# The last two of sixteen batches transposed by the DMA crossbar instead of TensorE

## Chip, cores, metric

One core of one Trainium2 chip. The metric is the device time of one execution in microseconds (us), as the runs report it.

## The reference

RWKV time mixing on x of 16 x 2048 x 256 (batch, sequence, model), fp32. Cut to what matters (the key branch is computed by the reference but never reaches the output):

```python
x_prev[:, 1:, :] = x[:, :-1, :]                  # the token before, zero for the first
xv = x * time_mix_v + x_prev * (1 - time_mix_v)
xr = x * time_mix_r + x_prev * (1 - time_mix_r)
v = xv @ value_weight
r = xr @ receptance_weight
out = (1 / (1 + exp(-r)) * v) @ output_weight
```

## The kernel before

The 32,768 tokens are worked in 64 units of 512, four to a batch. SBUF and PSUM are the two on-chip memories. For a unit, TensorE transposes x (tokens on partitions) so that the model dimension lies on partitions, ScalarE copies the result from PSUM to SBUF, VectorE and GpSimd mix each column with the column of the token before (a scale by a per-partition coefficient, then an add), and TensorE projects. The token before is in the neighbouring slot of 128 columns, which is why `xt` has one slot more than the batch; that first slot is filled by a "slot copy".

```python
def transposes(i):                       # runs LOOK = 6 units ahead
    ...
    ps = ps_t_pool.tile([P, KO, TU], BF16, name="ps_t")
    for ko in range(KO):                 # 8 TensorE transposes a unit
        one(ps[:, ko], ko, src, idn)
    nc.scalar.copy(out=xt[b][:, :, c0 : c0 + TU], in_=ps)
...
for g in range(NU - 1):                  # NU = 64 units
    project(ps_r, g, 0)                              # TensorE
    nc.scalar.activation(out=s_sb, in_=ps_r, func=ACT.Sigmoid)
    advance(START_T[g] if g < len(START_T) else g + LOOK)   # loads, transposes
    for p in products.get(g + 1, []):
        if g + LOOK >= NU and p[0][1] == 1:
            scale_act(p[0], (0,))        # value scale of a pair of units on ScalarE
    ...                                  # otherwise scales and adds on VectorE
    project(ps_v, g, 1)                              # TensorE
    nc.vector.tensor_tensor(out=z_sb, in0=s_sb, in1=ps_v, op=ALU.mult)
    for p in pooled[g]:
        scale_pool(p, last)              # the other half of the scales, GpSimd
    ...
    output(g - 1, z_prev)                # TensorE, copy on ScalarE, store by Sync
```

## Time and profile before

| | before |
|---|---|
| median of four runs | 212.62 us (212.14 to 213.71) |
| span of the profiled execution | 211.2 us |
| TensorE, VectorE, ScalarE busy | 96%, 91%, 89% of the span |
| pace in the middle | 3.046 us a unit |

A share of busy time says that three engines are nearly full, not which of them sets the pace. That is read from the idle time in front of each group of instructions; the prediction shows those lines. It also shows what units without TensorE transposes cost: 2.695 us, in the last units of this very kernel.

### The profile page before, as it was taken

How to read it: one execution, taken by the hardware profiler on the slowest of the kernel's cores; microseconds unless marked ns; L12 is line 12 of the kernel's file. 1: busy time of each engine (PE TensorE's matmuls, PEld its weight loads, DVE VectorE, ACT ScalarE, POOL GpSimd, SP SyncE). 2: the span in 40 equal slices, each digit the busy share in tenths (PEclk: the TensorE clock that was granted, in tenths of full speed). 3: DMA queues.
4: the chain of work that ended last, by engine and by line, in shares of the span. 5: the costliest groups of instructions: out<-in, count | busy, mean ns of one | idle time of the engine just before them, and what ended most of it. 6: DMA issues, size and time to landing. Idle time of an engine off the chain costs nothing.

```text
span 211.2 us, 4188 instructions
## 1 busy us (share of the span) xinstructions
PE 201.8 (96%) x1562; PEld 134.6 (64%) x1589; DVE 192.0 (91%) x314; ACT 187.2 (89%) x206; POOL 78.7 (37%) x108
## 2 busy tenths in 40 slices
PE   8879999999999999999999999999999999999991
PEld 7456665666666666666666666666666666665570
DVE  2869999999999999999999999999999999999962
ACT  3669999999999999999999999999999999999891
POOL 2623231544344425433452444335344432444200
PEclk9999999999999999999999999999999999999998
DMA  5999999999999897998989999898999944433475
GB/s 181 281 214 221 215 265 238 319 219 292 270 250 273 273 230 326 192 354 174 298 228 236 337 194 352 157 317 231 242 304 203 371 202 202 199 143 154 202 300 202
DMA packets 10284, 52.04 MB, mean 246 GB/s; under 512 B 1044, under 2 KB 2328, under 8 KB 5144
## 3 DMA queue, kind: packets, MB, share of 16 engines
q0 software_dynamic: 3008, 16.12, 44.2%
q1 hardware_dynamic: 7104, 35.52, 41.4%
q8 instruction: 12, 0.20, 0.4%
q10 hardware_dynamic: 152, 0.13, 0.2%
q14 instruction: 8, 0.07, 0.1%
HBM read 34.34 MB, written 33.55 MB: 322 GB/s over the span
## 4 chain that ended last, share of the span: by engine, by line
PE 79%; DVE 7%; DMA 5%; issue 4%; ACT 2%; POOL 1%; SPq 0%; DVEq 0%; POOLq 0%
PE psum_o L298 23%; PE psum_v L274 22%; PE psum_r L274 21%; PE ps_t L189 11%; DMA x_unit<-in_x_dram 5%; DVE mix L263 3%; DVE mix L239 2%; ACT s_sb L501 2%; DVE z_sb L527 1%; POOL mix L250 1%; PE ps_t L298 1%; ACT xt_first L206 0%; PE ps_t L274 0%; DVE xt_first L402 0%; DVE z_sb L359 0%
## 5 line engine op out<-in xcount | busy, mean ns | idle before, releaser
L250 POOL TENSOR_SCALAR mix<-xt,c_sb 128x1024 bf16<-128x1024 bf16 (+1 forms) x55 | 61.1, 1111 | 100.9 <-DVE mix L263 98.8
L527 DVE TENSOR_TENSOR z_sb<-s_sb,psum_v 128x1024 bf16<-128x1024 bf16 x63 | 76.7, 1218 | 4.7 <-PE psum_v L274 2.5
L263 DVE TENSOR_TENSOR mix<-mix,xt 128x1024 bf16<-128x1024 bf16 x112 | 78.0, 699 | 2.6
L330 ACT COPY o_sb<-psum_o 128x1024 f32<-128x1024 f32 x61 | 62.0, 1016 | 11.7 <-PE psum_o L298 11.7
L274 PEld LDWEIGHTS <-w_bf 128*128 128x128 bf16 x516 | 47.9, 98 | 33.8 <-issue 1.1
L501 ACT ACTIVATE s_sb<-psum_r 128x1024 bf16<-128x1024 f32 x63 | 65.1, 1034 | 0.5 <-PE psum_r L274 0.2
L274 PE MATMUL psum_v<-mix,w_bf 128*128 128x512 bf16 (+1 forms) x246 | 64.3, 377 | 0.8 <-DVE z_sb L527 0.2
L298 PE MATMUL psum_o<-wo_bf,z_sb 128*128 128x256 bf16 x498 | 64.8, 273 | 0.2
L274 PE MATMUL psum_r<-mix,w_bf 128*128 128x512 bf16 (+1 forms) x236 | 62.8, 377 | 0.6
L298 PEld LDWEIGHTS <-z_sb 128*128 128x128 bf16 x512 | 49.9, 98 | 20.2 <-DVE z_sb L359 1.2
L206 ACT COPY xt<-ps_t 128x1024 bf16<-128x1024 bf16 x56 | 57.0, 1022 | 0.0
L189 PEld LDWEIGHTS <-x_bf 128*128 128x128 bf16 x488 | 32.1, 98 | 13.5
L189 PE MATMUL ps_t<-ident,x_bf 128*128 128x128 bf16 x488 | 36.7, 219 | 0.2
L239 DVE TENSOR_SCALAR mix<-xt,c_sb 128x1024 bf16<-128x1024 bf16 (+1 forms) x59 | 26.9, 463 | 0.0
L263 DVE TENSOR_TENSOR mix<-mix,xt_first 128x1024 bf16<-128x1024 bf16 x15 | 10.2, 687 | 0.1
L250 POOL TENSOR_SCALAR mix<-xt_first,c_sb 128x512 bf16<-128x512 bf16 x6 | 4.1, 690 | 13.0 <-DVE xt_first L402 10.8
L106 POOL DMA_DIRECT2D x_bf<-in_x_dram x14 | 8.1, 582 | 0.0
L239 DVE TENSOR_SCALAR mix<-xt_first,c_sb 128x512 bf16<-128x512 bf16 x22 | 6.6, 349 | 0.2
L206 ACT COPY xt_first<-ps_t 128x1024 bf16<-128x1024 bf16 x5 | 5.2, 1033 | 0.0
L199 ACT CAST xt_first<-ps_t 128x512 bf16<-128x512 f32 x4 | 2.1, 589 | 3.3 <-PE ps_t L189 3.3
L140 PE MATMUL ps_t<-zeros 128*128 128x128 bf16 x38 | 3.8, 275 | 1.0 <-DVE zeros L84 1.0
L140 PEld LDWEIGHTS <-zeros 128*128 128x128 bf16 x38 | 3.2, 126 | 1.0 <-DVE zeros L84 1.0
(64 smaller groups left out, 43.4 us busy)
## 6 DMA issues: line engine op xcount, KB each, us to landing
out_dram<-o_sb SPq DMA_DIRECT2D x30, 1024.0 KB, 7.8
x_bf<-in_x_dram POOLq DMA_DIRECT2D x14, 1024.0 KB, 11.1
x_bf<-in_x_dram POOLq DMA_DIRECT2D x5, 256.0 KB, 8.8
x_unit<-in_x_dram SPq DMA_DIRECT2D x2, 512.0 KB, 6.3
out_dram<-o_sb SPq DMA_DIRECT2D x4, 256.0 KB, 2.1
x_unit<-in_x_dram SPq DMA_DIRECT2D x2, 256.0 KB, 3.0
out_dram<-o_sb SPq DMA_DIRECT2D x1, 512.0 KB, 2.6
out_dram<-o_sb SPq DMA_DIRECT2D x3, 128.0 KB, 2.7
```

What stands on the lines that cost most here:

```text
L106: nc.gpsimd.dma_start(out=x_bf[b], in_=rows(b))
L140: nc.tensor.matmul(out=ps, lhsT=zeros, rhs=zeros, start=True, stop=True)
L189: nc.tensor.transpose(out=ps[:, jj * P : (jj + 1) * P], in_=src[:, jj, ko * P : (ko + 1) * P], identity=idn,)
L206: nc.scalar.copy(out=xt[b][:, :, c0 : c0 + TU], in_=ps)
L239: nc.vector.tensor_scalar(out=mix[b][:, m, ko, lo:hi], in0=xt[b][:, ko, c : c + hi - lo], scalar1=c_sb[:, m, ko : ko + 1], scalar2=None, o ...
L250: op = nc.gpsimd.tensor_scalar(out=mix[b][:, m, 1, lo:hi], in0=xt[b][:, 1, c : c + hi - lo], scalar1=c_sb[:, m, 1:2], scalar2=1.0, op0=ALU ...
L263: return nc.vector.tensor_tensor(out=mix[b][:, m, :, lo:hi], in0=mix[b][:, m, :, lo:hi], in1=xt[b][:, :, c : c + hi - lo], op=ALU.add,)
L274: nc.tensor.matmul(out=ps[:, mo, :], lhsT=w_bf[:, m, ko, mo * P : (mo + 1) * P], rhs=mix[b][:, m, ko, e * TU + lo : e * TU + hi], start=(k ...
L298: nc.tensor.matmul(out=ps[:, slot, :], lhsT=z[:, ko, jj * P : (jj + 1) * P], rhs=wo_bf[:, ko, :], start=(ko == 0), stop=(ko == KO - 1),)
L330: nc.scalar.copy(out=o_sb[b][:, j0 : j0 + UJ, :], in_=ps)
L501: nc.scalar.activation(out=s_sb, in_=ps_r, func=ACT.Sigmoid)
L527: nc.vector.tensor_tensor(out=z_sb, in0=s_sb, in1=ps_v, op=ALU.mult)
```

## The change

Intent: TensorE sets the pace, and 0.45 us of each unit is transposes. Near the end the loads are done and the DMA engines have time, so the last two batches (units 56 to 63) are transposed by a DMA, SBUF to SBUF, one instruction for each batch (`dma_start_transpose`, called the crossbar below). The DMA writes block by block (token slot, then half of the model dimension), so `xt` and `mix` get that order in all batches. Batches 14 and 15 must lie whole in SBUF earlier, hence a fourth input buffer and loads two units earlier; to make room the first units' input shares an output buffer. ScalarE, rid of its copies, takes the value scale in those units.

```diff
+    BYDMA = 2
-    xpool = ctx.enter_context(tc.tile_pool(name="xpool", bufs=3))
+    xpool = ctx.enter_context(tc.tile_pool(name="xpool", bufs=4))
-    x_unit = consts.tile([P, 3, UJ, D], FP32)
+    x_unit = opool.tile([P, 3, UJ, D], FP32, name="o_sb")
-            xt[b] = xtpool.tile([P, KO, (J + 1) * P], BF16, name="xt")
+            xt[b] = xtpool.tile([P, J + 1, KO, P], BF16, name="xt")
+    def by_dma(b):
+        new_xt(b)
+        late_copies.append((b, UB - 1))
+        nc.sync.dma_start_transpose(
+            out=xt[b][:, 1:].rearrange("p j k c -> p (j k) c"),
+            in_=x_bf[b].rearrange("p j d -> p (j d)"),
+        )
... (all access patterns follow the new order)
-            if e == 1 and 2 < b + 2 < B:
-                load(b + 2)
-            transposes(tnext)
+            if e == UB - 1 and b + 3 < B:
+                load(b + 3)
+            if b < B - BYDMA:
+                transposes(tnext)
...
+        if g % UB == 0 and B - BYDMA <= g // UB + 2 < B:
+            by_dma(g // UB + 2)
-            if g + LOOK >= NU and p[0][1] == 1:
+            if g + LOOK >= NU - BYDMA * UB and p[0][1] == 1:
```

More of the change, by code (lines that the diff above doesn't have):

```diff
@@ L145, in new_xt @@
         if b < BYUNIT:
-            xt[b] = consts.tile([P, KO, UB * (UJ + 1) * P], BF16, name=f"xt_first{b}")
+            xt[b] = consts.tile([P, UB * (UJ + 1), KO, P], BF16, name=f"xt_first{b}")
         else:
-            xt[b] = xtpool.tile([P, KO, (J + 1) * P], BF16, name="xt")
-        (nc.vector if b == 0 else nc.gpsimd).memset(xt[b][:, :, 0:1], 0.0)
+            xt[b] = xtpool.tile([P, J + 1, KO, P], BF16, name="xt")
+        (nc.vector if b == 0 else nc.gpsimd).memset(xt[b][:, 0, :, 0:1], 0.0)
     new_xt(0)
@@ L182, in transposes, with one @@
             e = (e - 1) % UB
-        c0 = (1 + e * UJ + (e if b < BYUNIT else 0)) * P
+        j0 = 1 + e * UJ + (e if b < BYUNIT else 0)
         if b < BYUNIT or e == UB - 1:
             late_copies.append((b, e))
-        def one(ps, ko, src, idn):
-            for jj in range(UJ):
-                nc.tensor.transpose(
-                    out=ps[:, jj * P : (jj + 1) * P],
-                    in_=src[:, jj, ko * P : (ko + 1) * P],
-                    identity=idn,
-                )
+        def one(ps, jj, ko, src, idn):
+            nc.tensor.transpose(
+                out=ps[:, jj], in_=src[:, jj, ko * P : (ko + 1) * P], identity=idn
+            )
         if i in (1, 2):
             for ko in range(KO):
-                ps = ps_t_pool.tile([P, TU], FP32, name="ps_t")
-                one(ps, ko, x_unit[:, i], ident_f)
-                nc.scalar.copy(out=xt[b][:, ko, c0 : c0 + TU], in_=ps)
+                ps = ps_t_pool.tile([P, UJ, P], FP32, name="ps_t")
+                for jj in range(UJ):
+                    one(ps, jj, ko, x_unit[:, i], ident_f)
+                nc.scalar.copy(out=xt[b][:, j0 : j0 + UJ, ko, :], in_=ps)
             return
-        ps = ps_t_pool.tile([P, KO, TU], BF16, name="ps_t")
+        ps = ps_t_pool.tile([P, UJ, KO, P], BF16, name="ps_t")
         src = x_bf3 if b == 0 else x_bf[b][:, e * UJ : (e + 1) * UJ, :]
-        idn = ident
-        for ko in range(KO):
-            one(ps[:, ko], ko, src, idn)
-        nc.scalar.copy(out=xt[b][:, :, c0 : c0 + TU], in_=ps)
+        for jj in range(UJ):
+            for ko in range(KO):
+                one(ps[:, :, ko], jj, ko, src, ident)
+        nc.scalar.copy(out=xt[b][:, j0 : j0 + UJ], in_=ps)
     def first_transposes():
         def half(h, pool, name):
-            ps = pool.tile([P, KO, TU], FP32, name=name)
-            for ko in range(KO):
-                for jj in range(H):
+            ps = pool.tile([P, UJ, KO, P], FP32, name=name)
+            for jj in range(H):
+                for ko in range(KO):
                     nc.tensor.transpose(
-                        out=ps[:, ko, jj * P : (jj + 1) * P],
+                        out=ps[:, jj, ko],
                         in_=x_unit[:, 0, h * H + jj, ko * P : (ko + 1) * P],
@@ L217, in half @@
                     )
-            c0 = (1 + h * H) * P
-            nc.scalar.copy(out=xt[0][:, :, c0 : c0 + H * P], in_=ps[:, :, 0 : H * P])
+            nc.scalar.copy(out=xt[0][:, 1 + h * H : 1 + h * H + H], in_=ps[:, 0:H])
         pl = ps_t_pool.tile([P, KO, P], FP32, name="ps_t")
@@ L225, in first_transposes, with slots, mixed @@
             )
-        nc.vector.tensor_copy(out=xt[0][:, :, 1:P], in_=pl[:, :, 0 : P - 1])
+        nc.vector.tensor_copy(out=xt[0][:, 0, :, 1:P], in_=pl[:, :, 0 : P - 1])
         half(1, ps_r_pool, "psum_r")
         half(0, ps_v_pool, "psum_v")
-    def columns(piece):
-        b, _, lo, _ = piece
-        return lo + (lo // TU) * P if b < BYUNIT else lo
+    def slots(piece, off=0):
+        b, _, lo, hi = piece
+        j = lo // P + (lo // TU if b < BYUNIT else 0) + off
+        return slice(j, j + (hi - lo) // P)
+    def mixed(piece):
+        b, m, lo, hi = piece
+        return mix[b][:, m, lo // P : hi // P]
     def scale(piece, kos=(0, 1)):
-        b, m, lo, hi = piece
-        c = columns(piece)
+        b, m, _, _ = piece
         for ko in kos:
             nc.vector.tensor_scalar(
-                out=mix[b][:, m, ko, lo:hi],
-                in0=xt[b][:, ko, c : c + hi - lo],
+                out=mixed(piece)[:, :, ko],
+                in0=xt[b][:, slots(piece), ko],
                 scalar1=c_sb[:, m, ko : ko + 1],
@@ L247, in scale_pool @@
     def scale_pool(piece, after):
-        b, m, lo, hi = piece
-        c = columns(piece)
+        b, m, _, _ = piece
         op = nc.gpsimd.tensor_scalar(
-            out=mix[b][:, m, 1, lo:hi],
-            in0=xt[b][:, 1, c : c + hi - lo],
+            out=mixed(piece)[:, :, 1],
+            in0=xt[b][:, slots(piece), 1],
             scalar1=c_sb[:, m, 1:2],
@@ L260, in add @@
     def add(piece):
-        b, m, lo, hi = piece
-        c = columns(piece) + P
+        b = piece[0]
         return nc.vector.tensor_tensor(
-            out=mix[b][:, m, :, lo:hi],
-            in0=mix[b][:, m, :, lo:hi],
-            in1=xt[b][:, :, c : c + hi - lo],
-            op=ALU.add,
+            out=mixed(piece), in0=mixed(piece), in1=xt[b][:, slots(piece, 1)], op=ALU.add
         )
@@ L276, in project @@
                     lhsT=w_bf[:, m, ko, mo * P : (mo + 1) * P],
-                    rhs=mix[b][:, m, ko, e * TU + lo : e * TU + hi],
+                    rhs=mix[b][:, m, (e * TU + lo) // P : (e * TU + hi) // P, ko],
                     start=(ko == 0),
@@ L285, in project_unmixed @@
         parts = [(w_prev[:, ko], ko, 0) for ko in range(KO)]
-        parts += [(w_bf[:, 0, ko], ko, P) for ko in range(KO)]
+        parts += [(w_bf[:, 0, ko], ko, 1) for ko in range(KO)]
         for n, (w, ko, lo) in enumerate(parts):
@@ L290, in project_unmixed @@
                 lhsT=w[:, mo * P : (mo + 1) * P],
-                rhs=xt[0][:, ko, lo : lo + TU],
+                rhs=xt[0][:, lo : lo + UJ, ko],
                 start=(n == 0),
@@ L377, in tile_for @@
         if b not in mix:
-            mix[b] = mixpool.tile([P, 2, KO, J * P], BF16, name="mix")
+            mix[b] = mixpool.tile([P, 2, J, KO, P], BF16, name="mix")
     def pieces(g):
@@ L396, in wrap_slots @@
             late_copies.remove(key)
-        c = columns(piece) if by_unit else 0
-        n = (UJ if by_unit else J) * P
-        if by_unit and c > 0:
+        j = slots(piece).start if by_unit else 0
+        n = UJ if by_unit else J
+        if by_unit and j > 0:
             engine = nc.vector if key == (0, 1) else nc.gpsimd
-            engine.tensor_copy(out=xt[b][:, kos, c : c + 1], in_=xt[b][:, kos, c - 1 : c])
+            engine.tensor_copy(out=xt[b][:, j, kos, 0:1], in_=xt[b][:, j - 1, kos, P - 1 : P])
         nc.vector.tensor_copy(
-            out=xt[b][:, kos, c + 1 : c + P], in_=xt[b][:, kos, c + n : c + n + P - 1]
+            out=xt[b][:, j, kos, 1:P], in_=xt[b][:, j + n, kos, 0 : P - 1]
         )
@@ L477, in scale_act @@
     def scale_act(piece, kos):
-        b, m, lo, hi = piece
+        b, m, _, _ = piece
         for ko in kos:
             nc.scalar.activation(
-                out=mix[b][:, m, ko, lo:hi],
-                in_=xt[b][:, ko, columns(piece) : columns(piece) + hi - lo],
+                out=mixed(piece)[:, :, ko],
+                in_=xt[b][:, slots(piece), ko],
                 func=ACT.Copy,
@@ L514 @@
         for p, kos in products[g]:
-            if not (g - 1 + LOOK >= NU and p[1] == 1):
+            if not (g - 1 + LOOK >= NU - BYDMA * UB and p[1] == 1):
                 scale(p, kos)
```

## The prediction

> **What bounds the kernel now.** I read the page first (busy times, slices), then the groups of instructions by shape in a steady stretch, then the timeline of single units, then the DMA view. A "unit" below is 512 of the 32,768 tokens; there are 64 of them, numbered by g.
>
> ```profile
> PE 201.8 (96%) x1562; PEld 134.6 (64%) x1589; DVE 192.0 (91%) x314; ACT 187.2 (89%) x206; POOL 78.7 (37%) x108
> ...
> PE   8879999999999999999999999999999999999991
> ...
> DMA  5999999999999897998989999898999944433475
> ```
>
> TensorE is busy from end to end, VectorE and ScalarE are only a few per cent behind it. The DMA engines are full until about slice 32 of 40 (169 us) and then fall to four tenths: the last input load is done, only stores are left. The chain of waits agrees with a TensorE bound: 79% of it is PE.
>
> The groups in the stretch from 100 to 142.65 us, which holds 14 units of 3.046 us:
>
> ```profile
> L263 DVE TENSOR_TENSOR mix<-mix,xt 128x1024 bf16<-128x1024 bf16 x29 | 20.3, 699 | 0.7
> L527 DVE TENSOR_TENSOR z_sb<-s_sb,psum_v 128x1024 bf16<-128x1024 bf16 x14 | 17.1, 1220 | 1.3 <-PE psum_v L274 0.9
> L250 POOL TENSOR_SCALAR mix<-xt,c_sb 128x1024 bf16<-128x1024 bf16 x14 | 15.7, 1119 | 25.4 <-DVE mix L263 25.4
> ...
> L206 ACT COPY xt<-ps_t 128x1024 bf16<-128x1024 bf16 x15 | 15.3, 1018 | 0.0
> ...
> L330 ACT COPY o_sb<-psum_o 128x1024 f32<-128x1024 f32 x14 | 14.2, 1013 | 2.9 <-PE psum_o L298 2.9
> ...
> L189 PE MATMUL ps_t<-ident,x_bf 128*128 128x128 bf16 x112 | 8.5, 219 | 0.1
> ```
>
> The last column is what to see. TensorE's groups wait 0.1 us in 14 units; ScalarE waits 0.2 us per unit for TensorE (2.9 over 14), VectorE 0.1. So TensorE sets 3.046 us per unit, and the other two have about 0.2 us of slack each. The pieces of the chain give TensorE's unit: 0.86 (psum_r) + 0.45 (eight transposes) + 0.86 (psum_v) + 0.87 (psum_o) = 3.04 us. The 219 ns of one transpose is its latency; the pitch is 0.45/8 = 0.056 us.
>
> The kernel already shows what a unit without transposes costs. Transposes run six units ahead (LOOK), so units 58 to 62 have none:
>
> ```profile
> 190.21 1.03 PE L274 MATMUL psum_v<-mix,w_bf 128*128 128x512 bf16 x4
> ...
> 191.37 1.15 ACT L480 ACTIVATE mix<-xt,c_sb 128x1024 bf16<-128x1024 bf16 x1
> ...
> 192.41 1.01 ACT L330 COPY o_sb<-psum_o 128x1024 f32<-128x1024 f32 x1
> ...
> 192.86 1.02 PE L274 MATMUL psum_v<-mix,w_bf 128*128 128x512 bf16 x4
> ...
> 193.31 1.05 ACT L501 ACTIVATE s_sb<-psum_r 128x1024 bf16<-128x1024 f32 x1
> ...
> 194.38 1.22 DVE L527 TENSOR_TENSOR z_sb<-s_sb,psum_v 128x1024 bf16<-128x1024 bf16 x1 [0.36 <-ACT s_sb L501]
> ```
>
> The starts of psum_v in that view are 190.21, 192.86, 195.66, 198.39 and 200.99: a mean of 10.78/4 = 2.695 us, not the 2.60 that TensorE alone would need. The lines show why: in every second unit ScalarE has a scale (1.15) between the sigmoid and the output copy, the next sigmoid starts late, and VectorE waits 0.36 us for it. VectorE is itself near its limit: start to start, product 1.14, two adds 0.60 each, and a scale of 0.40 in every second unit, 2.74 us in such a unit.
>
> **What the Trainium skill says.** (1) "TensorE: Matmul & The Clock Gate", Part 4: PE-mode transpose: about 275 ns for 128x128 in one kernel's context, result in PSUM, so a copy must follow. The trace has 219 ns of latency, and the copy is the 1018 ns ScalarE row above. (2) "VectorE: DVE Perf Modes", The three transpose paths: the crossbar takes 1309 ns for one 128x128 and writes SBUF directly, so no copy is needed. The kernel before has no such instruction. (3) "DMA: Bandwidth & Descriptors", Latency and other measured facts: a transposing DMA reaches 261 GB/s with a non-contiguous middle dimension, some 350 to 400 otherwise; its rules table adds that a transpose next to ordinary DMAs needs nothing. No run yet shows it. (4) "SBUF — State Buffer", Who interferes with whom: a VectorE instruction with two SBUF inputs contends with a GpSimd one that reads SBUF. In this trace the 1.12 us GpSimd scale lies under the product (1.22 us, one input in PSUM), and adds stay at 0.68 to 0.78 us, so the kernel already avoids it.
>
> **The change, part by part.**
>
> Transposes of batches 14 and 15 (units 56 to 63). They are issued in units g = 50 to 57, so eight units lose them. Removed: 64 TensorE transposes, 8 x 0.45 = 3.6 us of TensorE's path; 8 ScalarE copies of 1.02 us. ScalarE takes in exchange the value scale of four pairs (units 50, 52, 54, 56), 4 x 1.15 = 4.6 us, which leaves VectorE (4 x 0.48 us). Per unit that is the mix of work of units 58 to 62 of the kernel before, so I take their pace: 8 x (3.046 - 2.695) = **2.8 us saved**, less than TensorE's 3.6, because ScalarE and VectorE take over at 2.70.
>
> Two crossbar transposes of 1 MiB. They cost nothing if they land before VectorE's slot copy, the first reader. In the kernel before those copies are at 175.25 us (batch 14, g = 53) and 187.44 us (batch 15, g = 57); in the shortened stretch about 174.2 and 185.0. Sync works in order, so the transposes come after the stores of g = 46 (about 157.1 us) and g = 50 (169.26 us). The first may also wait for GpSimd's clearing of column 0, queued behind its scale that ends at 159.5 us. Room: about 15 to 17 us each. At 261 GB/s, an estimate from the skill's figure, 1.05 MB takes 4.0 us, plus some 2 us to land (a 256 KB store lands in 2.1). Even with stores between, 6 to 9 us: hidden. Their inputs are there: loads are now called for two units earlier (6 us), so batch 15 is requested near 150 us instead of 156.28 and lands 10 to 15 us later, before 166.
>
> Fourth input buffer, x_unit in an output buffer: no path. GpSimd issues as many loads of 0.58 us; the shared buffer is next written by the third batch's output, long after the first units' transposes.
>
> Slot-wise tiles: the scales, the matmuls' moving operand and GpSimd's scale read runs of 128 elements (256 B) instead of 512 or 1024; adds and ScalarE's copy become contiguous. Same counts, same elements; I expect every mean within 2%, zero effect. This touches all 64 units, so it is the part where a small error would cost most: 0.1 us on GpSimd or VectorE disappears in slack of 0.2 us, 0.3 us would not.
>
> Sum: 212.8 - 2.8 = 210.0; I add 0.2 for small losses (start-up, where VectorE and not TensorE sets the pace): **210.2 us**.
>
> **The rivals.**
>
> A, the crossbar is slow. One instruction covers 32 blocks; at 1309 ns each with no overlap that is 42 us, some 26 us over the room, and the kernel would end near 235 us or above. For it: nothing in the trace says that blocks overlap. Against: 1309 ns for 32 KB is mostly a fixed time if a stream reaches 261 GB/s. In between: the table of sequencer cycles in the same DMA page gives earlier generations 262,144 cycles for 8,192 tiles in SBUF, 32 each. If a tile is 2 to 4 KB (my estimate, the table names no size), 1 MiB has 256 to 512 tiles, at the 1.2 GHz that the skill's overview ("Trainium Kernel Development and Optimization") gives Sync 7 to 14 us, plus landing 9 to 16: just at the edge, a stall of 0 to 3 us, 210 to 213 us.
>
> B, the layout slows a hot instruction. If runs of 256 B made GpSimd's scale outlast the product it lies under (1.12 against 1.22 us), VectorE's adds would be pushed back, the 0.2 us of slack would go, and each further 0.1 us would cost some 5 us over the steady stretch: 213 to 218. Against: the innermost step stays 1 and the number of slots even.
>
> C, TensorE's whole 3.6 us is saved, because ScalarE without copies has caught up and uneven units average out: 209.2 us. Against: units 58 to 62 had the same mix and did not reach 2.60.
>
> D, the transposes delay the stores behind them in Sync's queue. There are three output buffers and 24 us until one is rewritten; hidden unless A holds.
>
> **Range and chances.** The mechanism says 209.2 (C) to 210.5; I give it 70%. Rival A's middle form and a mild B, 211 to 215, get 17%; a long stall or a bad layout, over 217, 13%. More than 2% faster means below 208.6 us, 4.3 us saved, which even TensorE's 3.6 does not reach. Range 209.2 to 214.0. Faster 0.05, same 0.81, slower 0.14.
>
> **What would show it.** Right: TensorE's transposes fall by 64, ScalarE's xt copies by 8, the value scales on ScalarE rise by 4; psum_v starts are 3.05 us apart up to g = 49 and about 2.70 after; the slot copy waits for no DMA. Wrong: an idle VectorE before the slot copies with a DMA as releaser (A), a steady pace other than 3.05 us or a GpSimd scale well over 1.12 us (B), 2.60 us per unit near the end (C), ScalarE waiting to write an output buffer (D).

## The result

The changed kernel takes 209.82 us (median of four runs, 209.41 to 210.11), before 212.62; the ratio is 0.986, interval 0.982 to 0.990. A ratio here is the mean time of one kernel's fast runs over that of the other's of the same rounds, so it isn't quite the ratio of the medians. It was repeated on another occasion: 209.09 beside 212.46, ratio 0.985.

Three groups of the page before, then the groups of the page after, whole execution (count, busy us, mean ns, then idle time before and what ended it):

```profile
L250 POOL TENSOR_SCALAR mix<-xt,c_sb 128x1024 bf16<-128x1024 bf16 (+1 forms) x55 | 61.1, 1111 | 100.9 <-DVE mix L263 98.8
...
L206 ACT COPY xt<-ps_t 128x1024 bf16<-128x1024 bf16 x56 | 57.0, 1022 | 0.0
...
L189 PE MATMUL ps_t<-ident,x_bf 128*128 128x128 bf16 x488 | 36.7, 219 | 0.2
```

```profile
L260 POOL TENSOR_SCALAR mix<-xt,c_sb 128x1024 bf16<-128x1024 bf16 (+1 forms) x55 | 61.0, 1108 | 98.1 <-DVE mix L272 93.7
L536 DVE TENSOR_TENSOR z_sb<-s_sb,psum_v 128x1024 bf16<-128x1024 bf16 x63 | 76.7, 1217 | 4.2 <-PE psum_v L280 1.8
L272 DVE TENSOR_TENSOR mix<-mix,xt 128x1024 bf16<-128x1024 bf16 x112 | 78.1, 701 | 2.2
...
L214 ACT COPY xt<-ps_t 128x1024 bf16<-128x1024 bf16 x48 | 48.9, 1024 | 0.0
...
L198 PE MATMUL ps_t<-ident,x_bf 128*128 128x128 bf16 x424 | 31.8, 219 | 0.0
...
L487 ACT ACTIVATE mix<-xt,c_sb 128x1024 bf16<-128x1024 bf16 x6 | 6.9, 1149 | 0.0
```

Before, the same rows counted 488 TensorE transposes and 56 copies; 64 and 8 are gone, and the ScalarE scales rose from 2 to 6. GpSimd's scale and VectorE's operations kept their means, so runs of 256 bytes did not lengthen them.

The timeline after, around the second transpose (start us, duration, engine):

```profile
164.63 1.03 PE L280 MATMUL psum_v<-mix,w_bf 128*128 128x512 bf16 x4
...
165.79 1.15 ACT L487 ACTIVATE mix<-xt,c_sb 128x1024 bf16<-128x1024 bf16 x1
...
167.27 1.02 PE L280 MATMUL psum_v<-mix,w_bf 128*128 128x512 bf16 x4
...
168.36 7.15 SPq L181 DMA_TRANSPOSE xt<-x_bf  x1
...
168.79 1.22 DVE L536 TENSOR_TENSOR z_sb<-s_sb,psum_v 128x1024 bf16<-128x1024 bf16 x1 [0.35 <-ACT s_sb L508]
...
170.07 1.02 PE L280 MATMUL psum_v<-mix,w_bf 128*128 128x512 bf16 x4
...
173.29 0.21 DVE L408 COPY xt<-xt 128x254 bf16<-128x254 bf16 x1
```

The last line is batch 14's slot copy. It has no bracket: it waited for nothing. Its transpose was issued at 156.37 us, held Sync for 8.63 us and landed 10.7 us after issue, at 167.1, 6.2 us before it was needed. The second was issued at 168.36; if it took as long it landed at 179.1, 5.0 us before the copy at 184.06.

The starts of psum_v in that timeline go from 164.63 (unit 50) to 186.17 (unit 58): 21.54/8 = 2.69 us a unit, where before they went from 166.29 to 190.21, with 3.045 up to unit 57. The eight steps that lost their transposes are those from unit 49 to unit 57: 21.54 us after (162.03 to 183.57), 24.37 before (163.24 to 187.61), 2.83 less. The spans of the two profiles differ by more, 3.6 us; the rest is a start-up that was 1.2 us shorter in this one execution (see below) and an end that was 0.5 us longer.

### The profile page after: what moved, and what is told of

Read it like the earlier page. It is cut to its first block, busy times and chain, and to the rows that moved or that the text cites. A ratio compares the mean times of both kernels' runs of the same rounds, so it can differ in the third digit from the quotient of the medians.

```text
span 207.6 us, 4083 instructions
## 1 busy us (share of the span) xinstructions
PE 201.1 (97%) x1525; PEld 132.0 (64%) x1525; DVE 189.8 (91%) x310; ACT 183.6 (88%) x202; POOL 78.7 (38%) x108
## 4 chain that ended last, share of the span: by engine, by line
PE 83%; DVE 6%; ACT 4%; DMA 2%; issue 2%; POOL 1%; SPq 0%; DVEq 0%; POOLq 0%
PE psum_v L280 24%; PE psum_o L304 24%; PE psum_r L280 23%; PE ps_t L198 10%; DMA w_f<-n_receptance_weight_dram 2%; DVE mix L272 2%; DVE mix L250 2%; ACT s_sb L508 1%; PE psum_r L294 1%; ACT xt_first L214 1%; POOL mix L260 1%; DVE z_sb L536 1%; ACT mix L487 1%; PE ps_t L304 1%; ACT xt_first L207 0%
## 5 line engine op out<-in xcount | busy, mean ns | idle before, releaser
L280 PE MATMUL psum_v<-mix,w_bf 128*128 128x512 bf16 (+1 forms) x256 | 65.3, 377 | 0.3 <-DVE z_sb L536 0.2
L280 PE MATMUL psum_r<-mix,w_bf 128*128 128x512 bf16 (+1 forms) x252 | 64.3, 377 | 0.0
L214 ACT COPY xt<-ps_t 128x1024 bf16<-128x1024 bf16 x48 | 48.9, 1024 | 0.0
L198 PEld LDWEIGHTS <-x_bf 128*128 128x128 bf16 x424 | 27.9, 98 | 11.6
L198 PE MATMUL ps_t<-ident,x_bf 128*128 128x128 bf16 x424 | 31.8, 219 | 0.0
L250 DVE TENSOR_SCALAR mix<-xt,c_sb 128x1024 bf16<-128x1024 bf16 (+1 forms) x55 | 24.9, 461 | 0.0
L272 DVE TENSOR_TENSOR mix<-mix,xt_first 128x1024 bf16<-128x1024 bf16 x15 | 10.2, 688 | 0.1
L260 POOL TENSOR_SCALAR mix<-xt_first,c_sb 128x512 bf16<-128x512 bf16 x6 | 4.1, 688 | 13.3 <-DVE xt_first L408 10.9
L487 ACT ACTIVATE mix<-xt,c_sb 128x1024 bf16<-128x1024 bf16 x6 | 6.9, 1149 | 0.0
```

What stands on the lines that cost most here:

```text
L198: nc.tensor.transpose(out=ps[:, jj], in_=src[:, jj, ko * P : (ko + 1) * P], identity=idn)
L214: nc.scalar.copy(out=xt[b][:, j0 : j0 + UJ], in_=ps)
L250: nc.vector.tensor_scalar(out=mixed(piece)[:, :, ko], in0=xt[b][:, slots(piece), ko], scalar1=c_sb[:, m, ko : ko + 1], scalar2=None, op0=A ...
L260: op = nc.gpsimd.tensor_scalar(out=mixed(piece)[:, :, 1], in0=xt[b][:, slots(piece), 1], scalar1=c_sb[:, m, 1:2], scalar2=1.0, op0=ALU.mul ...
L272: return nc.vector.tensor_tensor(out=mixed(piece), in0=mixed(piece), in1=xt[b][:, slots(piece, 1)], op=ALU.add)
L280: nc.tensor.matmul(out=ps[:, mo, :], lhsT=w_bf[:, m, ko, mo * P : (mo + 1) * P], rhs=mix[b][:, m, (e * TU + lo) // P : (e * TU + hi) // P, ...
```

## The experiments

Twelve kernels ran, all correct against the reference but one; each "before" is the kernel before on the same chip in the same rounds.

### No batch through the crossbar; one; three; four

The number of batches is one constant (`BYDMA`), the rest of the change stays.

```diff
-    BYDMA = 2
+    BYDMA = 0        # then 1, 3, 4
```

> No batch goes through the crossbar (all 64 units transposed by TensorE), everything else of the change kept: slot-wise tiles, four input buffers, first units' input in an output buffer, loads two units earlier. Theory (the gain is the eight transposes-free units, 2.8 us, the rest costs nothing): within 0.3% of the kernel before, 212.2 to 213.2 us, steady pace 3.046 us, GpSimd scale 1.11 to 1.12 us. Rival (the start-up, which in the one profile after is 1.2 us ahead of the one before, is part of the gain): 211.2 to 211.8 us, with unit 49's psum_v again near 162.0 us instead of 163.2.

> Only batch 15 through the crossbar. Theory (each unit without TensorE transposes saves 3.046 - 2.69 = 0.355 us): four units, 1.4 us less than with none, 1.4 us more than with two batches: 211.2 us where before is 212.6. Rival (the gain is a fixed one from start-up and end, not proportional to batches): the same time as the changed kernel, 209.8 us.

> Batches 13, 14 and 15 through the crossbar. The changed kernel's queue row for Sync grew from 41.4% of 211.2 us to 48.1% of 207.6 us, 12.4 us of all 16 engines for two transposes, 6.2 us each. Theory 1 (DMA engines have a little room while loads still run): 1.4 us faster than two batches, 208.4 us where before is 212.6. Theory 2 (they are full until 163 us, share 0.92 to 1.0, so a third transpose pushes the last loads and the following transposes back by some 6 us and past their room of 5 us): no gain or a loss, 209.8 to 213 us, with VectorE's slot copy waiting for a DMA.

> Batches 12 to 15 through the crossbar. Theory 1 (room): 207.0 us where before is 212.6. Theory 2 (DMA engines full): 12 us of added DMA work before the last loads, so that the transposes of batches 14 and 15 land some 7 us late: 211 to 218 us, slot copies waiting for DMA, transposes taking over 11 us to land.

| batches | median us | ratio to before (211.94 here) | span of the profile |
|---|---|---|---|
| 0 | 212.44 (212.19 to 214.41) | 1.003, 0.9997 to 1.0067 | 210.4 |
| 1 | 210.71 (209.25 to 211.09) | 0.992, 0.989 to 0.995 | 209.1 |
| 2 (earlier) | 209.82 | 0.986, 0.982 to 0.990 | 207.6 |
| 3 | 223.45 (214.85 to 229.73) | none, see below | 227.9 |
| 4 | 227.01 (215.76 to 230.82) | none, see below | 217.6 |

With none, nothing is gained: layout, buffers and earlier loads are worth nothing by themselves, and if anything cost 0.3% (the interval reaches 0.7%). So the start-up lead in the profiled executions (unit 49's psum_v at 162.03 us after, 163.24 before) isn't a part of the gain. In the profiled execution of before, TensorE waited 1.7 us for the third unit's input; in the profile with no batch by DMA psum_v of unit 49 was at 162.43, and that kernel is no faster. One batch gives 1.3 us of span, two give 2.8, and in the profile with one batch the four steps from unit 53 to 57 take 10.77 us (174.58 to 185.35) instead of 12.18 before, 1.41 less: the gain goes with the number of units without transposes, as the theory says. The ratios alone show this less well: the first batch is worth some 2.3 us by them and the second some 1.3 to 1.5, each known to about 0.7.

Three batches are far slower, which neither theory had in this size. The executions scatter so much that the profiled ones count as slow (over 1.5% above the fastest of their kernel), so no ratio is formed; that even the fastest of six (214.85) is slower than the slowest of the eleven runs before (212.86) is what I use. The granted clock doesn't explain it: in the page's slices it is full until the stall described next and low only after it. Where it went stands in the waits of the profile with three (engine, line, waited for: us in total, times, longest):

```profile
PE psum_v L280 <- DVE z_sb L536: 19.4, 2, 19.1
DVE xt L408 <- DMA xt<-x_bf: 19.3, 1, 19.3
```

VectorE's slot copy waited 19.3 us for a transpose, and everything behind it stood. Sync's timeline of the same run:

```profile
144.60 12.81 SPq L181 DMA_TRANSPOSE xt<-x_bf  x1
...
158.67 28.63 SPq L181 DMA_TRANSPOSE xt<-x_bf  x1
...
188.57 9.39 SPq L181 DMA_TRANSPOSE xt<-x_bf  x1
```

The first landed after 36.3 us, at 180.9, just when the slot copy that had waited 19.3 us started; the third landed after 11.0; for the second the trace has no landing. Between the first and the second, batch 15's load was issued at 149.28 and took 31.3 us to land. The DMA view from 156 to 160 us of that run (packets, then each queue's packets, MB and share of the 16 engines' time; q1 carries transposes and stores, q0 the loads):

```profile
DMA packets 92, 0.08 MB, mean 20 GB/s; under 512 B 85, under 2 KB 85, under 8 KB 85
...
q1 hardware_dynamic: 84, 0.02, 95.1%
q0 software_dynamic: 8, 0.06, 14.6%
```

And from 162 to 166 us of the changed kernel, the first transpose's packets with no load in flight:

```profile
DMA packets 3278, 0.85 MB, mean 214 GB/s; under 512 B 3276, under 2 KB 3276, under 8 KB 3276
...
q1 hardware_dynamic: 3278, 0.85, 118.9%
```

Same kind of packets (under 512 B), same stretch of 4 us, but 20 against 214 GB/s. In both views the queue's packets are in flight nearly all the time; in the first they hardly move. The difference to see is q0: load packets between those of the transpose. Two transposes in flight at once are not what starts it: from 150 to 154 us, with no load packet moving, the first transpose moved over 1000 packets in each 2 us, from 156 to 158, after the load's first packets, 41, and the second transpose was issued only at 158.67. With four batches it is the same: the first transpose took 18.0 us, the second, issued 12 us after it, 26.5, and in the 2 us from 143 to 145 us four transpose packets and four load packets moved.

### The result again, a plain copy, and where the scales go

> The changed kernel once more, as reference for the three beside it: 0.986 of the kernel before, as measured; no theory differs.

209.09 us (208.52 to 210.57), before 212.46: ratio 0.9853, 0.9821 to 0.9885.

```diff
-        nc.sync.dma_start_transpose(
-            out=xt[b][:, 1:].rearrange("p j k c -> p (j k) c"),
+        nc.sync.dma_start(
+            out=xt[b][:, 1:].rearrange("p j k c -> p (j k c)"),
```

> Wrong result on purpose: each crossbar transpose replaced by a plain copy of the same 1 MiB from the same to the same tile on the same queue. Theory (the transposes are hidden, 5 to 6 us before the slot copy that needs them): same time as the changed kernel within 0.3%, though Sync is held less than 1 us instead of 7 to 9 us for each. Rival (the crossbar costs something, by memory traffic or by holding back stores): 0.5 us or more faster.

209.43 us, ratio 0.9870 (0.9839 to 0.9900), result wrong as meant. Sync is held 0.71 and 0.47 us instead of 8.88 and 7.43 (the repeat's transposes), a copy lands in 9.5 us instead of 10.7, and the time is the same. The crossbar costs the path nothing; the theory holds.

```diff
-            if g + LOOK >= NU - BYDMA * UB and p[0][1] == 1:
+            if g + LOOK >= NU and p[0][1] == 1:
-            if not (g - 1 + LOOK >= NU - BYDMA * UB and p[1] == 1):
+            if not (g - 1 + LOOK >= NU and p[1] == 1):
```

> The four value scales of units 50 to 56 stay on VectorE (0.48 us each) instead of going to ScalarE (1.15 us each). Theory (VectorE and ScalarE share the limit): every unit then has a scale on VectorE, start to start 1.14 + 0.60 + 0.60 + 0.40 = 2.74 us, against 2.69 now: 0.4 us slower than the changed kernel. Rival (ScalarE alone holds the tail at 2.69, so without its scale TensorE's 2.60 shows): 0.7 us faster.

211.30 us, ratio 0.9937 (0.9900 to 0.9973): about 1.8 us slower than the changed kernel beside it, not 0.4; in the profile, whose span is 1.0 us longer, 2.885 us a unit from unit 50 to 58 (164.39 to 187.47) instead of 2.69. The direction was right, the size was not, and VectorE's timeline shows why:

```profile
176.43 0.47 DVE L250 TENSOR_SCALAR mix<-xt,c_sb 128x1024 bf16<-128x1024 bf16 x1
176.83 0.68 DVE L272 TENSOR_TENSOR mix<-mix,xt 128x1024 bf16<-128x1024 bf16 x1
177.43 1.21 DVE L536 TENSOR_TENSOR z_sb<-s_sb,psum_v 128x1024 bf16<-128x1024 bf16 x1
178.56 0.70 DVE L272 TENSOR_TENSOR mix<-mix,xt 128x1024 bf16<-128x1024 bf16 x1
179.18 0.48 DVE L250 TENSOR_SCALAR mix<-xt,c_sb 128x1024 bf16<-128x1024 bf16 x1
179.76 0.69 DVE L272 TENSOR_TENSOR mix<-mix,xt 128x1024 bf16<-128x1024 bf16 x1
```

From scale to add it is 0.40 us at 176.43, but 0.58 at 179.18: the second is a value scale, which the very next add reads, while the first is read by a later add. I had taken 0.40 for both, which accounts for 0.09 of the 0.145 us by which 2.885 exceeds my 2.74; the rest is the slot copy in every fourth unit (0.14 us from its start to the next) and adds that take 0.63 to 0.70 us start to start after a product, where I had 0.60. VectorE is without a gap, so it alone sets 2.885 here. Without moving the scale to ScalarE most of the gain would have been lost: this small edit is worth more than half of the change.

```diff
             group = (b, m, lo, hi + TU if paired else hi)
+            if u - 2 + LOOK >= NU - BYDMA * UB:
+                products[w].append(((b, m, lo, hi), (0,)))
+                products[w + 1].append(((b, m, hi, hi + TU), (0,)))
+                pooled[w - 1].append(group)
+                continue
```

> From unit 50 on each scale of a pair of units is split in two halves of 512 columns, one in each unit, on VectorE and on ScalarE. Theory (the tail runs at 2.69 and not 2.60 because both scales fall in every second unit): VectorE 1.14 + 0.60 + 0.60 + 0.27 = 2.61, ScalarE 0.92 + 0.90 + 0.64 = 2.46, so TensorE's 2.60 to 2.62 a unit; over units 50 to 62 some 0.9 us faster than the changed kernel. Rival (the tail is held by the wait chain between engines within a unit, not by load): no change, 2.69.

208.45 us, ratio 0.9826 (0.9797 to 0.9855). The intervals overlap with the changed kernel's, but the profile says the same as the medians: from unit 49 to 62, 34.33 us (162.02 to 196.35) instead of 34.91 (162.03 to 196.94), 0.58 us less. ScalarE and VectorE in one unit of it:

```profile
177.10 1.01 ACT L336 COPY o_sb<-psum_o 128x1024 f32<-128x1024 f32 x1 [0.20 <-PE psum_o L304]
...
178.03 1.02 ACT L513 ACTIVATE s_sb<-psum_r 128x1024 bf16<-128x1024 f32 x1
...
178.34 0.34 DVE L250 TENSOR_SCALAR mix<-xt,c_sb 128x512 bf16<-128x512 bf16 x1
...
178.95 0.71 ACT L492 ACTIVATE mix<-xt,c_sb 128x512 bf16<-128x512 bf16 x1
```

ScalarE now waits for TensorE again (0.20). Paces of 2.60 to 2.62 appear as expected, but units with a slot copy and the one after stay at 2.75 and 2.68, where VectorE has no gap; so 0.6 of the expected 0.9 us.

### Room and collision

```diff
-        if g % UB == 0 and B - BYDMA <= g // UB + 2 < B:
+        if g % UB == 3 and B - BYDMA <= g // UB + 2 < B:
```

> The two crossbar transposes are put one store later in Sync's order (behind the stores of units 49 and 53), about 12 us later. They land 10.7 us after issue and had 5 to 6 us of room. Theory (they cost nothing only because they land before VectorE's slot copy): the copies of units 53 and 57 wait 5 to 6 us each, 219 to 221 us where before is 212.5. Rival (something else covers it, the queues run ahead): under 212 us.

219.47 us, ratio 1.033 (1.028 to 1.038): the theory's time. From the view of line 408 in its profile, what the slot copies waited for:

```profile
  DMA xt<-x_bf: 6.7, 2
```

The two waits are 3.9 and 2.8 us, shorter than expected because the first transpose landed in 8.8 us (issued at 169.19, well after the last load). They cost more than their length: TensorE stood still, in gaps of 3.69 and 2.61 us, and the granted clock was 0.63 from 178 to 182 us and 0.52 from 182 to 186 (1.00 before and after), then 0.76 from 194 to 198 and 0.85 from 198 to 203. So missing the deadline by 3 or 4 us costs about 5 each, and the room of 5 to 6 us is what makes the change free.

```diff
             by_dma(g // UB + 2)
+        if g == 51:
+            nc.gpsimd.dma_start(out=x_bf[12], in_=rows(12))        # or
+            nc.scalar.dma_start(out=x_bf[12], in_=x_bf[13])
```

> The changed kernel with one more input load (batch 12 again, 1 MiB with the cast, on GpSimd's queue, into its own finished buffer) issued in unit 51, so that it runs beside the second crossbar transpose. In the run with three batches the transpose issued beside a load took 36 us to land, and the DMA engines moved 20 to 110 GB/s for 20 us. Theory (transpose packets and the casting load hold each other up on the 16 engines): the second transpose lands after 20 us or more, slot copy waits, 215 us or more. Rival (three batches failed because the sum of DMA work did not fit): the load adds 6 us of DMA work in a stretch that is less than half busy, the transpose lands within 16 us, the time stays within 0.5% of the changed kernel.

> As the run with the extra load, but the extra transfer is a plain copy of 1 MiB from SBUF to SBUF on ScalarE's hardware queue. Theory (it is the casting load of the GpSimd queue that collides): the transpose lands within 16 us, time within 0.7% of the changed kernel (0.4 us of ScalarE for the issue). Rival (any other queue's packets between those of the transpose do it): 20 us or more to land and 215 us or more.

210.05 us (ratio 0.9887, 0.9842 to 0.9932) with the load, 209.74 (0.9874, 0.9832 to 0.9916) with the copy. The theory's prediction for the load failed: no slot copy waited, though Sync was held 13.37 us by the second transpose (7.15 without a load). But the trace shows that the trial missed the state it was to make. The load was in flight from 168 to 180 us, while q1 was still moving the store ahead of the transpose; in the 8 us from 170 to 178 only 16 packets under 512 B went, and the bulk of the short packets (1154, 1137 and 1749 in three stretches of 2 us from 178) came when the load had 25 packets of 0.07 MB left. The load delayed the transpose rather than interleaving with it. So it neither shows nor refutes a collision of the two kinds of packets. The trial with the copy missed it too: its packets (q10) moved from 168 to 173.5 us and none after, while 1725 of the transpose's short packets went from 173.5 to 176. The landing moved to 13.3 us at most and nothing was lost, but this doesn't show that another queue's copy is harmless beside a transpose.

```diff
-    xpool = ctx.enter_context(tc.tile_pool(name="xpool", bufs=4))
+    xpool = ctx.enter_context(tc.tile_pool(name="xpool", bufs=5))
-    BYDMA = 2
+    BYDMA = 3
-            if e == UB - 1 and b + 3 < B:
-                load(b + 3)
+            if (b, e) == (0, UB - 1):
+                load(3)
+            if b and e == UB - 1 and b + 4 < B or (b, e) == (1, 1):
+                load(b + 4 if e == UB - 1 else 4)
```

> Three batches through the crossbar as in the run that was slow, but five input buffers and each load called four units (12 us) earlier, so that the last load is done near 148 to 150 us and the second and third transposes (issued at 156 and 168 us) run beside no load; the first (144.6 us) still meets the end of one. Theory (collision with loads is the cause): 208.0 to 209.5 us where before is 212.5, transposes landing in 11 to 24 us. Rival (total DMA work is the cause, or the first transpose's collision alone is enough): 212 us or more.

208.39 us (207.91 to 208.92), before 212.28, ratio 0.9813 (0.9781 to 0.9845). Sync's timeline, to set against that of the slow run:

```profile
144.18 8.38 SPq L181 DMA_TRANSPOSE xt<-x_bf  x1
...
156.18 7.09 SPq L181 DMA_TRANSPOSE xt<-x_bf  x1
...
166.95 7.78 SPq L181 DMA_TRANSPOSE xt<-x_bf  x1
```

The same three transposes, issued at the same times as far as nothing held them up, with the same bytes in total; only the last load is done (it was issued at 136.67 and landed 10.1 us later) before the bulk of the first transpose's short packets begins (32 went from 144 to 148 us, 491 from 148 to 150). The two landings that the trace has took 10.2 and 9.4 us (first and third), and no slot copy waited. The sum of DMA work, the rival, is therefore not what broke the run with three batches: when the loads run is.

The same trace hints that loads may not be the only packets that do this. From 162 to 166 us one packet of the instruction queue (q8) went, and the second transpose nearly stopped, at 8 to 13 GB/s or less from 163.7 to 164.9; from 170 to 174 us, and in the late-issue run from 172 to 176, no other queue had a packet and there was no such stop. No experiment tested it.

This version and the one with split scales both beat the changed kernel by the medians, by less than their intervals separate; a kernel with both edits was not run.

## Why the prediction was right

**TensorE sets the pace, so eight units without transposes gain.** Right, by the runs with none, one and two batches.

**Pace of units 58 to 62 taken for units 50 to 57, 8 x (3.046 - 2.695) = 2.8 us.** Measured 2.69, 2.83 us less over the eight steps, and a gain of 2.8 us in the medians (3.4 in the repeat). TensorE's own 3.6 us (rival C) was not reached, for the reason given: splitting the scales moved most units to 2.60. The prediction called VectorE near its limit, at 2.74 us in a unit with a scale; it is nearer. With the value scale left on VectorE the pace is 2.885, in larger part because a scale whose result the next add reads takes 0.58 us of VectorE's order and not 0.40.

**The transposes are hidden.** Right, shown by the plain copy that changes nothing and by the late issue that costs 10 us. The size was off: I estimated 6 to 9 us to land, it was 10.7, and Sync was held for 7.15 to 8.63 us. The middle form of rival A, from the skill's table of sequencer cycles and my guess of a tile's size (an estimate: 7 to 14 us of Sync, 9 to 16 to land), described it better; only the room, estimated at 15 to 17 us and measured as 16.9 and 15.7 (issue to slot copy), kept it from costing anything.

**Layout and buffers: no effect.** Right as far as is known: the run with no batch is 0.3% slower, interval 0.0 to 0.7%, with equal means. Rival B did not occur.

**Start-up, 0.2 us lost.** Not resolved; it is within the scatter.

**Not seen.** That earlier loads were a condition and not a detail. I checked only that a batch is there when its transpose is issued. The run with three batches, against the one with the same three and loads 12 us earlier, shows that what counts also is that no load is left when the transpose's short packets go. Why the two kinds of packets bring the engines to 20 GB/s stays open: that they were in flight together in each long slow stretch is seen in two runs, and that keeping them apart cures it in one; the two trials that set out to provoke it did not bring the packets together.

## What to carry to other kernels

Moving work off the engine that sets the pace gains only down to the next engine's pace: find a stretch of the present kernel that already has the new mix of work and take its pace, and move some work of the next engine in the same change. A DMA that takes over an engine's work has a deadline, so work out issue, landing and first reader, and leave room: a miss also costs TensorE's clock. Let large casting loads end before a crossbar transpose begins.

## What the Trainium skill lacked or had wrong

- "DMA: Bandwidth & Descriptors", DMA Transpose: no time for which one instruction holds the issuing queue; the page's table of sequencer cycles counts in tiles of a size that the table doesn't give. Here 1 MiB from SBUF to SBUF (128 x 4096 bf16) held Sync for 7.0 to 10.0 us with no load beside it or only the end of one, and landed in 8.8 to 11.9. The page's 261 GB/s, by which I estimated 4.0 us, can describe the packets alone: in the 4 us shown they moved at 214 GB/s, a pause of 1.2 us included.
- The same page, Rules for kernel authors, says that a transpose next to ordinary DMAs needs nothing. All results with a transpose were right, so it holds for the data; of the time it says nothing, and here it was 20 GB/s beside a casting load, and 36.3 us to land.
- "VectorE: DVE Perf Modes", The DRAIN you can't avoid: no figure for what a dependence on the operation just before costs. Here a scale to the add after it is 0.40 us start to start, 0.58 when the add reads that scale.
- "TensorE: Matmul & The Clock Gate", Why this matters for your kernels, warns of idle gaps of TensorE over some 3 us. The late-issue run agrees for a gap of 3.69 us (granted clock down to 0.52 in a view of 4 us), but a gap of 2.61 us, under the page's figure, was followed by a lower clock too (0.76).
